# Which loads a pair of weight buffers is kept for, and one weight unit moved ahead of a block, in a hybrid decoder block on one core

## The chip, the cores and the metric

The kernel runs on one core of one Trainium2 chip. The metric is the device time of one execution in microseconds. The time before is the median of three runs, 1735.49 us (1733.80 to 1738.36).

## The reference, cut to what matters

One decoder layer on 256 tokens of width 2048, in fp32: a SwiGLU feed-forward, a mixer, and a second SwiGLU feed-forward, each on a normalised input and added to the residual, and a last norm. The change lies in the two feed-forwards, whose three weights have a hidden width of 5632.

```python
def swiglu_ffn(x, w_gate, w_up, w_down):
    return (jax.nn.silu(x @ w_gate) * (x @ w_up)) @ w_down

x = x + 0.5 * swiglu_ffn(rms_norm(x, ffn1_norm), ffn1_w_gate, ffn1_w_up, ffn1_w_down)
z = rms_norm(x, mix_norm) @ w_in
...  # convolutions, a linear recurrence, gates: y
x = x + y @ w_out
x = x + 0.5 * swiglu_ffn(rms_norm(x, ffn2_norm), ffn2_w_gate, ffn2_w_up, ffn2_w_down)
return rms_norm(x, final_norm)
```

## The kernel before

Every product of activations and weights is made in three passes of TensorE (PE): an fp32 operand is split into a high part (`hi`, a cast by ScalarE, ACT) and a low part (`lo`, the difference to the high part, by VectorE, DVE), and hi·hi, lo·hi and hi·lo are added up. Activations stand still in the array, weights stream through it. A **unit** of weights is 512 rows by 512 columns, 1 MB, in a tile of 128 x 4 x 512. It is loaded by SyncE's queue (SP) into a `raw` buffer, cast in two halves of 128x1024 by ACT, subtracted as 128x2048 by DVE, and then gives 24 matmuls of 128x512: 16 with the high part, 8 with the low one.

There are two ways to use weights. A **plain unit** (`unit`, then `multiply`) is used as just told. A **block** (`seven`) takes two by two units and needs seven products for them where eight are usual; each is made of one sum or difference of weights (by DVE, in place in the raw buffer) and one of activations. Its products come in the order p0, p4, p5, p6, p2, p3, p1, and its four sums lie in the PSUM banks `a`, `c`, `e` and `d`. The weights are w11, w12, w21, w22. p0 uses w11 itself; then DVE writes w12 - w11 into w11's buffer for p4, then w22 less that for p5, and w22 - w12 into w12's buffer for p6. Rows outside the two by two are added by `usual` steps (`x01`, `x00`), which use the units `b2`, `a2` and so on.

A feed-forward runs its hidden width in five double columns, s = 0 to 4, after a first single column. For each s come a gate block and an up block (tiles `g` and `u` with the number of s), and for s = 0, 2 and 4 a **down stage** (tile `d`), which brings the hidden units that are ready back to the width of 2048. In the first down stage these are three, 0, 1 and 2: `others` is [0] and (m, n) is (1, 2). In the two later ones there are four each. A down stage covers output columns 1 and 2 with a block over (m, n) and columns 0 and 3 with plain units, written (column, unit) here. In the first stage their order is (0,0), (0,2), (3,0), (0,1), the block, (3,2), (3,1).

Raw buffers come from two pools. `raws` has three and serves everything; `more` (tag `kept`) has two, is there while a feed-forward runs, and holds w11 and w12 of the blocks. The rule for plain units is the one the diff touches:

```python
        if kept is None and extra and not turn_of["hold"]:
            turn_of["raw"] += 1
            kept = turn_of["raw"] % 5 > 2
```

`unit` passes `kept=None`, so that in down stages two plain units of every five go to the `kept` pair. A load waits until its buffer is free, and SP issues its loads in order. The parts `hi` and `lo` have three pairs of buffers in a feed-forward.

`seven` has an argument `whole`. If it is true, p0's bank `a` is copied by ACT into bank `d`, where the last product goes on adding; if not, ACT copies it into a kept tile `s1`, and DVE adds it at the end. The up block of s = 0 has it false.

The order of the instructions on each engine is set by a scheduler when the kernel is built, so the order in the code is not always that of an engine. All engine operations are recorded at one line, L43, the loads at L168 (`load`) and the transposes at L436. Groups are told apart by tiles: `ps_d_a<-lo_d_p,hs` is a matmul of a down block into bank a, with the low part of the weights of a product p and a sum `hs` of activations; `hi_d` and `lo_d` without a letter behind are plain units.

Of the kernel before, what the change touches and what calls it, by code (L numbers as in the profile page):

```python
# [49 lines left out]
def hybrid_block(ctx: ExitStack, tc: tile.TileContext, a: dict, out: bass.AP):  # L50
# [16 lines left out]
    def pump(budget):  # L67

        owed[0] = min(owed[0], 0.0) + budget
        while pending and owed[0] > 0:  # L70
            cost, fn = pending.popleft()
            fn()
            owed[0] -= cost
# [9 lines left out]
    def bank(name):  # L83
        return psum.tile([P, 512], F32, tag="ps", name=name)

    def f32(ap):
        return ap.bitcast(F32)
# [66 lines left out]


    extra = []
    turn_of = {"raw": 0, "split": 0, "hold": False}

    def load(src, name, pieces=((0, UK),), loaded=None, kept=False):
        if kept is None and extra and not turn_of["hold"]:  # L160
            turn_of["raw"] += 1
            kept = turn_of["raw"] % 5 > 2
        if kept:
            raw = extra[1].tile([P, UK, CW], F32, tag="kept", name=f"raw_{name}", bufs=2)
        else:
            raw = raws.tile([P, UK, CW], F32, tag="raw", name=f"raw_{name}")
        for i, e in pieces:
            nc.sync.dma_start(raw[:, i:e, :], src[i * P : e * P].rearrange("(j p) c -> p j c", p=P))  # L168
            if loaded:
                loaded(i)  # L170
        return raw

    def parts_of(raw, name, pieces=((0, 2), (2, UK)), split=None):
        pool, bufs = splits, 2
        if extra:
            turn_of["split"] += 1
            if turn_of["split"] % 3 == 0:
                pool, bufs = extra[0], 1
        hi = pool.tile([P, UK, CW], F32R, tag="hi", name=f"hi_{name}", bufs=bufs)
        lo = pool.tile([P, UK, CW], F32R, tag="lo", name=f"lo_{name}", bufs=bufs)  # L180
        for i, e in pieces:
            if split:
                split(i)
            act.copy(hi[:, i:e, :], raw[:, i:e, :])
            if split:
                dve.tensor_tensor(lo[:, i:e, :], raw[:, i:e, :], f32(hi[:, i:e, :]), op=ALU.subtract)
        if not split:
            dve.tensor_tensor(lo, raw, f32(hi), op=ALU.subtract)
        return [(hi[:, j, :], lo[:, j, :]) for j in range(UK)]

    def unit(src, name):
        return parts_of(load(src, name, kept=None), name)

    def stationary(tile, t):

        return [(tile[:, j, t * P : (t + 1) * P], tile[:, j, S + t * P : S + (t + 1) * P]) for j in range(UK)]
# [148 lines left out]
    def quad(tile):  # L345
        return tile.rearrange("p (j c) -> p j c", j=UK)
# [65 lines left out]
    def ffn(tag, norm, after, opening=False):  # L412
        with (
# [1 line left out]
            tc.tile_pool(name=f"more{tag}", bufs=1, side="right") as mp,  # L415
        ):
            extra.extend((fp, mp))
            turn_of["hold"] = True
            wg, wu, wd = (a[f"ffn{tag}_w_{s}"][0] for s in ("gate", "up", "down"))

            def keep(name, dt=F32):
# [46 lines left out]
            def on_the_way():  # L468
                return [*tiles, *(entry[0] for entry in moving)]
# [3 lines left out]
            units, vs, sf, ready = [], {}, {}, []  # L473
# [196 lines left out]

            (begin if opening else begin_after)()
            xs = list(enumerate(units))[2:]
            turn_of["hold"] = False

            def down(last):
                us = sorted(set(hidden) | {tile[0] for tile in on_the_way()})
                others, (m, n) = us[:-2], us[-2:]
                end = last and tag == 2

                def update(c, t, *parts):  # L680
                    xr = xres[:, t, c * CW : (c + 1) * CW]
                    for p in parts:
                        dve.scalar_tensor_tensor(xr, p, 0.5, xr, op0=ALU.mult, op1=ALU.add)
                    if last:
                        after(c, t)

                side = {c: [bank(f"ps_d{tag}_{m}_{c}_{t}") for t in range(NT)] for c in (0, 3)}

                def add_units(c, units):
                    blks = [  # L690
                        (u, unit(wd[u * UK * P : (u + 1) * UK * P, c * CW : (c + 1) * CW], f"d{tag}_{m}_{c}_{u}"))
                        for u in units
                    ]
                    assert not {tile[0] for tile in on_the_way()} & set(units)
                    groups = [[0], [1]] if end and units == [n, m] else [[0, 1]]
                    for ts in groups:
                        for u, blk in blks:
                            multiply(
                                [(side[c][t], stationary(hidden[u], t), u == us[0], u == m) for t in ts], blk
                            )  # L700
                            pump(1.5 / len(groups))
                    if units[-1] == m and not (end and c == 0):
                        Engine.pinned = end
                        for t in range(NT):
                            update(c, t, side[c][t])

                sh, got, rest = {}, {}, []

                def block_sums():
                    return seven_of(  # L710
                        sh, hidden[m], hidden[n],
                        {(t, i): turned[u, t] for t in range(NT) for i, u in ((0, m), (1, n))},
                        quad(keep(f"hspare{tag}_{m}")),
                        [[quad(keep(f"hs{tag}_{m}_{i}_{z}", F32R)) for z in range(2)] for i in range(4)],
                    )

                def add(t, b, ps, tiles):
                    got[t, b] = [ps] + tiles
                    if (0, b) in got and (1, b) in got:
                        for i in range(NT):  # L720
                            update(2 - b, i, *got[i, b])

                for c, u in [(0, u) for u in others + [n]] + [(3, u) for u in others]:
                    add_units(c, [u])
                    if not on_the_way() and not rest:
                        rest.append(block_sums())
                add_units(0, [m])

                def within(i):
                    if i == 0:  # L730
                        rest.pop()()
                    elif i == 1 and end:
                        for t in range(NT):
                            update(0, t, side[0][t])

                if tag == 1 and m == 5:
                    prepare()
                seven(
                    wd, (m, n), (2 * CW, CW), sh, [(u, hidden[u]) for u in others], f"d{tag}_{m}", keep, add,
                    within,  # L740
                )
                for units in [[n, m]] if end else [[n], [m]]:
                    add_units(3, units)
                hidden.clear()
                turned.clear()

            for s in range(5):
                cs = (CW + 2 * s * CW, 2 * CW + 2 * s * CW)
                sg = {}

                def total(ps, tiles):
                    for p in tiles[1:]:
                        dve.tensor_tensor(tiles[0], tiles[0], p, op=ALU.add)
                    if not tiles:
                        return ps
                    dve.tensor_tensor(tiles[0], ps, tiles[0], op=ALU.add)
                    return tiles[0]

                def gate(t, n, ps, tiles):
                    g = total(ps, tiles)  # L760
                    sg[t, n] = tiles[0] if tiles else keep(f"z{tag}_{s}")
                    act.activation(sg[t, n], g, AF.Silu)

                def up(t, n, ps, tiles):
                    dve.tensor_tensor(sg[t, n], total(ps, tiles), sg[t, n], op=ALU.mult)
                    turn_hidden(1 + 2 * s + n, t, sg[t, n], s % 2 == 0)

                def meanwhile(i):
                    if s == 0 and not opening and i != 1:
                        (sums, lambda: normalise(3))[i // 2]()  # L770

                seven(wg, (0, 1), cs, sf, xs, f"g{tag}_{s}", keep, gate, meanwhile, ready.pop() if ready else None,
                      s > 0 and (tag, s) != (1, 3))
                seven(wu, (0, 1), cs, sf, xs, f"u{tag}_{s}", keep, up, whole=s > 0)
                if s % 2 == 0:
                    down(s == 4)
            extra.clear()
# [45 lines left out]
    with tc.tile_pool(name="mixer", bufs=1) as mp, tc.tile_pool(name="mixw", bufs=2) as mw:  # L823
# [197 lines left out]
        for c in range(NC_D):  # L1021
            cs = slice(c * CW, (c + 1) * CW)
# [96 lines left out]
```

## Time and profile before

| | before |
|---|---|
| median of 3 runs | 1735.49 us (1733.80 to 1738.36) |
| the profiled execution | 1735.05 us |
| its span, mean granted clock of PE | 1733.1 us, 0.998 |
| PE, PE's weight loads | 99%, 82% of the span |
| DVE, ACT | 85%, 66% |
| moved by DMA | 354.75 MB, mean 205 GB/s |

The span is the time from the first to the last instruction of the profiled execution; the execution is longer by what lies around it. Shares are busy time over the span. A line of the timeline has its start, its length, the engine, the line of the code, the operation, the tile written and those read, the shape, how many instructions were joined (x), and in brackets how long the engine had been idle before and on whom it waited. In SP's lines the length is the time from the issue to the landing of the joined loads.

### The profile page before, as it was taken

The numbers are of one execution on the slowest core, as the hardware profiler recorded it, in microseconds if no ns is written. First come the engines' busy times: TensorE is split into PE (matmuls) and PEld (weight loads), VectorE is DVE, ScalarE is ACT, GpSimd is POOL, SyncE is SP. The second block draws the span as 40 slices with busy tenths as digits, with TensorE's granted clock in tenths as the row PEclk, the third lists the DMA queues.
The fourth block names the chain that finished last, engine by engine and source line by source line (L and its number), as shares of the span: only waits on it lengthen the run. The fifth ranks groups of instructions, "written<-read, shape, count | busy, mean of one in ns | idle before, by whom it ended". The sixth has DMA issues, their size and how long they took to land. (4 is left out here: it accounts for less than half of the span.)

```text
span 1733.1 us, 20143 instructions
## 1 busy us (share of the span) xinstructions
PE 1708.6 (99%) x7859; PEld 1417.9 (82%) x7859; DVE 1472.5 (85%) x1212; ACT 1136.4 (66%) x1433; POOL 6.9 (0%) x32
## 2 busy tenths in 40 slices
PE   8999999999999999999999999999999999999998
PEld 6888788888888888888888888787787887888886
DVE  7997998979799878687986668989799878889786
ACT  6867567775568676575655556686567665567764
POOL 1000000000000000000000000000000000000000
PEclk9999999999999999999999999999999999999999
DMA  8666557585567684556556664684577657576853
GB/s 297 203 217 185 202 199 217 197 266 194 186 211 232 212 249 152 191 170 194 179 187 207 226 200 134 214 264 164 179 233 227 203 187 243 194 213 200 242 202 114
DMA packets 220383, 354.75 MB, mean 205 GB/s; under 512 B 52100, under 2 KB 54528, under 8 KB 220160
## 3 DMA queue, kind: packets, MB, share of 16 engines
q1 hardware_dynamic: 219824, 352.36, 62.8%
q8 instruction: 61, 1.00, 0.2%
q10 hardware_dynamic: 144, 1.05, 0.1%
q14 instruction: 34, 0.28, 0.0%
q0 software_dynamic: 320, 0.07, 0.0%
HBM read 339.82 MB, written 2.10 MB: 197 GB/s over the span
## 5 line engine op out<-in xcount | busy, mean ns | idle before, releaser
L43 DVE TENSOR_TENSOR lo_u_p<-raw_u,hi_u_p 128x2048 fp32r<-128x2048 f32 x70 | 159.3, 2287 | 20.5 <-ACT hi_u_p L43 20.1
L43 ACT CAST hi_u_p<-raw_u 128x1024 fp32r<-128x1024 f32 x140 | 141.8, 1047 | 53.3 <-DVE raw_u L43 16.8
L43 DVE TENSOR_TENSOR lo_g_p<-raw_g,hi_g_p 128x2048 fp32r<-128x2048 f32 x66 | 150.1, 2286 | 25.0 <-ACT hi_g_p L43 24.9
L43 ACT CAST hi_g_p<-raw_g 128x1024 fp32r<-128x1024 f32 x132 | 132.7, 1047 | 54.6 <-DVE raw_g L43 28.6
L43 PE MATMUL ps_d<-hi_d,h 128*128 128x512 f32 x704 | 167.4, 389 | 0.0
L43 PEld LDWEIGHTS ps_d<-hi_d,h 128*128 128x128 f32 x704 | 132.0, 188 | 27.7 <-DVE h L43 0.3
L43 PE MATMUL ps_in<-xT_nm,hi_in 128*128 128x512 f32 x640 | 153.8, 391 | 0.0
L43 ACT CAST hi_d_p<-raw_d 128x1024 fp32r<-128x1024 f32 x84 | 85.4, 1047 | 77.6 <-DVE raw_d L43 34.2
L43 PEld LDWEIGHTS ps_in<-xT_nm,hi_in 128*128 128x128 f32 x640 | 117.3, 188 | 22.9 <-ACT tha L43 0.4
L43 DVE TENSOR_TENSOR lo_d<-raw_d,hi_d 128x2048 fp32r<-128x2048 f32 x44 | 100.4, 2289 | 32.7 <-ACT hi_d L43 32.6
L43 ACT CAST hi_in<-raw_in 128x1024 fp32r<-128x1024 f32 x80 | 80.0, 1045 | 66.3 <-PE ps_in L43 45.9
L43 DVE TENSOR_TENSOR lo_in<-raw_in,hi_in 128x2048 fp32r<-128x2048 f32 x40 | 91.4, 2287 | 35.3 <-ACT hi_in L43 32.9
L43 ACT CAST hi_u_x<-raw_u 128x1024 fp32r<-128x1024 f32 x80 | 80.9, 1046 | 46.5 <-PE ps_u_c L43 23.2
L43 DVE TENSOR_TENSOR lo_d_p<-raw_d,hi_d_p 128x2048 fp32r<-128x2048 f32 x42 | 95.9, 2287 | 15.3 <-ACT hi_d_p L43 15.3
L43 DVE TENSOR_TENSOR raw_u<-raw_u,raw_u 128x2048 f32<-128x2048 f32 x40 | 91.6, 2290 | 13.5 <-DMA raw_u<-in_ffn_w_up_dram 12.9
L43 ACT CAST hi_d<-raw_d 128x1024 fp32r<-128x1024 f32 x88 | 88.5, 1045 | 22.3 <-PE ps_d_d L43 9.8
L43 ACT CAST hi_g_x<-raw_g 128x1024 fp32r<-128x1024 f32 x80 | 81.1, 1046 | 31.7 <-PE ps_g_c L43 11.5
L43 DVE TENSOR_TENSOR lo_g_x<-raw_g,hi_g_x 128x2048 fp32r<-128x2048 f32 x40 | 91.4, 2286 | 2.4 <-ACT hi_g_x L43 2.1
L43 DVE TENSOR_TENSOR lo_u_x<-raw_u,hi_u_x 128x2048 fp32r<-128x2048 f32 x40 | 91.5, 2287 | 2.2 <-ACT hi_u_x L43 2.1
L43 DVE TENSOR_TENSOR raw_g<-raw_g,raw_g 128x2048 f32<-128x2048 f32 x37 | 84.5, 2287 | 7.6 <-DMA raw_g<-in_ffn_w_gate_dram 7.3
L43 PE MATMUL ps_d<-lo_d,h 128*128 128x512 f32 x352 | 87.3, 389 | 0.0
L43 PEld LDWEIGHTS ps_in<-xT_nm,lo_in 128*128 128x128 f32 x640 | 82.2, 191 | 3.2
(395 smaller groups left out, 3650.4 us busy)
## 6 DMA issues: line engine op xcount, KB each, us to landing
raw_d<-in_ffn_w_down_dram SPq DMA_DIRECT2D x88, 1024.0 KB, 5.4
raw_u<-in_ffn_w_up_dram SPq DMA_DIRECT2D x87, 1024.0 KB, 5.3
raw_g<-in_ffn_w_gate_dram SPq DMA_DIRECT2D x86, 1024.0 KB, 5.4
raw_in<-in_w_in_dram SPq DMA_DIRECT2D x40, 1024.0 KB, 5.1
raw_o<-in_w_out_dram SPq DMA_DIRECT2D x16, 1024.0 KB, 5.1
xres<-in_x_dram SPq DMA_DIRECT2D x4, 512.0 KB, 7.6
raw_u<-in_ffn_w_up_dram SPq DMA_DIRECT2D x2, 512.0 KB, 9.4
raw_g_first<-in_ffn_w_gate_dram SPq DMA_DIRECT2D x1, 1024.0 KB, 12.1
```

Source lines behind the costliest of these rows:

```text
L43: ins = getattr(self.engine, name)(*args, **kwargs)
```

## The change

Three things change. The rule above goes: plain units always take one of the three buffers of `raws`, and the `kept` pair holds w11 and w12 of blocks alone. In a down stage with one other unit, which is the first one of each feed-forward, the unit (3, n) stands ahead of the block in the place of behind it. And the up block of s = 0 takes the default `whole=True`, the copy into bank `d`. Line numbers after the first hunk move by three or four: loads are at L165 and transposes at L432.

```diff
@@ -154,12 +154,9 @@
     extra = []
-    turn_of = {"raw": 0, "split": 0, "hold": False}
+    turn_of = {"split": 0}
 
     def load(src, name, pieces=((0, UK),), loaded=None, kept=False):
-        if kept is None and extra and not turn_of["hold"]:
-            turn_of["raw"] += 1
-            kept = turn_of["raw"] % 5 > 2
         if kept:
...
     def unit(src, name):
-        return parts_of(load(src, name, kept=None), name)
+        return parts_of(load(src, name), name)
...
-            turn_of["hold"] = True
...
-            turn_of["hold"] = False
...
-                for c, u in [(0, u) for u in others + [n]] + [(3, u) for u in others]:
+                ahead = [n] if len(others) == 1 else []
+                for c, u in [(0, u) for u in others + [n]] + [(3, u) for u in others + ahead]:
                     add_units(c, [u])
...
-                for units in [[n, m]] if end else [[n], [m]]:
+                for units in [[n, m]] if end else [[u] for u in (n, m) if u not in ahead]:
                     add_units(3, units)
...
-                seven(wu, (0, 1), cs, sf, xs, f"u{tag}_{s}", keep, up, whole=s > 0)
+                seven(wu, (0, 1), cs, sf, xs, f"u{tag}_{s}", keep, up)
```

On PE, before, in the first feed-forward's first down stage from the unit (3,0) to the block's p0 (`ps_d1_1_3_0` is the bank of column 3 for the first half of the tokens, `hi_d1_1_3_0` the high part of unit 0 of column 3; the last number only numbers the tiles):

```order
L43 MATMUL ps_d1_1_3_0_1145<-hi_d1_1_3_0_1226,h1_0_708 128x512 x8
L43 MATMUL ps_d1_1_3_1_1146<-hi_d1_1_3_0_1226,h1_0_708 128x512 x8
L43 MATMUL ps_d1_1_3_0_1145<-lo_d1_1_3_0_1227,h1_0_708 128x512 x4
L43 MATMUL ps_d1_1_3_1_1146<-lo_d1_1_3_0_1227,h1_0_708 128x512 x4
L43 MATMUL ps_d1_1_0_0_1143<-hi_d1_1_0_1_1273,h1_1_1216 128x512 x8
L43 MATMUL ps_d1_1_0_1_1144<-hi_d1_1_0_1_1273,h1_1_1216 128x512 x8
L43 MATMUL ps_d1_1_0_0_1143<-lo_d1_1_0_1_1274,h1_1_1216 128x512 x4
L43 MATMUL ps_d1_1_0_1_1144<-lo_d1_1_0_1_1274,h1_1_1216 128x512 x4
L43 MATMUL ps_d1_1_a_1304<-hi_d1_1_p0_1320,h1_1_1216 128x512 x8
```

And after, from the end of the unit (3,0) on:

```order
L43 MATMUL ps_d1_1_3_1_1144<-lo_d1_1_3_0_1225,h1_0_708 128x512 x4
L43 MATMUL ps_d1_1_3_0_1143<-hi_d1_1_3_2_1271,h1_2_1114 128x512 x8
L43 MATMUL ps_d1_1_3_1_1144<-hi_d1_1_3_2_1271,h1_2_1114 128x512 x8
L43 MATMUL ps_d1_1_3_0_1143<-lo_d1_1_3_2_1272,h1_2_1114 128x512 x4
L43 MATMUL ps_d1_1_3_1_1144<-lo_d1_1_3_2_1272,h1_2_1114 128x512 x4
L43 MATMUL ps_d1_1_0_0_1141<-hi_d1_1_0_1_1302,h1_1_1214 128x512 x8
L43 MATMUL ps_d1_1_0_1_1142<-hi_d1_1_0_1_1302,h1_1_1214 128x512 x8
L43 MATMUL ps_d1_1_0_0_1141<-lo_d1_1_0_1_1303,h1_1_1214 128x512 x4
L43 MATMUL ps_d1_1_0_1_1142<-lo_d1_1_0_1_1303,h1_1_1214 128x512 x4
L43 MATMUL ps_d1_1_a_1333<-hi_d1_1_p0_1349,h1_1_1214 128x512 x8
```

The 24 matmuls of (3,2) now stand between (3,0) and (0,1); behind the block only (3,1) is left.

On SP, before, the loads of the second feed-forward's down stage of s = 2 (`raw_d2_5_0_3` is the plain unit (0,3), `raw_d2_5_50` and `raw_d2_5_51` are the block's w11 and w12, `raw_d2_5_31` its b2, `raw_d2_5_61` its w22):

```order
L168 DMA raw_d2_5_0_6_10593<-in_ffn2_w_down_dram 128x4x512
L436 DMA_TRANSPOSE u2_g2_2_10048<-plane2_10490 128x8x128
L168 DMA raw_d2_5_3_3_10640<-in_ffn2_w_down_dram 128x4x512
L168 DMA raw_d2_5_0_5_10702<-in_ffn2_w_down_dram 128x4x512
L436 DMA_TRANSPOSE z2_2_10207<-plane2_10551 128x8x128
L436 DMA_TRANSPOSE z2_2_10226<-plane2_10590 128x8x128
L168 DMA raw_d2_5_31_10743<-in_ffn2_w_down_dram 128x4x512
L168 DMA raw_d2_5_61_10745<-in_ffn2_w_down_dram 128x4x512
L168 DMA raw_d2_5_41_10747<-in_ffn2_w_down_dram 128x4x512
L168 DMA raw_d2_5_50_10739<-in_ffn2_w_down_dram 128x4x512
L168 DMA raw_d2_5_51_10741<-in_ffn2_w_down_dram 128x4x512
```

And after, the start of the same stage:

```order
L165 DMA raw_d2_5_50_10735<-in_ffn2_w_down_dram 128x4x512
L165 DMA raw_u2_2_30_10242<-in_ffn2_w_up_dram 128x4x512
L165 DMA raw_d2_5_0_3_10512<-in_ffn2_w_down_dram 128x4x512
L165 DMA raw_d2_5_51_10737<-in_ffn2_w_down_dram 128x4x512
L432 DMA_TRANSPOSE u3_g2_2_10100<-plane2_10431 128x8x128
L165 DMA raw_d2_5_0_4_10550<-in_ffn2_w_down_dram 128x4x512
L432 DMA_TRANSPOSE u2_g2_2_10044<-plane2_10486 128x8x128
```

The block's two first weights were the last of these to be issued and are now the first, ahead of and next to the stage's first plain unit.

## The prediction

> **What bounds the kernel now.** I read the page first, for the engine that has no room, then the waits of TensorE's weight loads, then busy time and clock by stretches of 50 us, and last the timeline where those two show a loss.
>
> ```profile
> PE 1708.6 (99%) x7859; PEld 1417.9 (82%) x7859; DVE 1472.5 (85%) x1212; ACT 1136.4 (66%) x1433; POOL 6.9 (0%) x32
> core 0: 1733.1 us, clock 0.998
> ```
>
> TensorE (PE) is busy 99% of the span, so only time in which PE stands still or runs slowly can be won. The span is 1733.1 us and the execution took 1735.05, so 1.95 us lie around it; I carry the sum in the execution's own time, which is 0.44 us below the median of 1735.49. The pace of PE is read from two starts:
>
> ```profile
> 151.01 3.79 PE L43 MATMUL ps_d<-hi_d,h 128*128 128x512 f32 x16
> 154.64 1.98 PE L43 MATMUL ps_d<-lo_d,h 128*128 128x512 f32 x8
> ```
>
> Sixteen matmuls take 154.64 - 151.01 = 3.63 us, 0.227 each. A plain unit has 16 + 8 of them, 5.44 us. The list of the waits (total us, count, mean us) names who keeps PE waiting there:
>
> ```profile
> PEld ps_d_a L43 <- DVE lo_d_p L43: 3.8, 2, 1.9
> PEld ps_d_c L43 <- ACT s_d L43: 3.1, 2, 2.2
> ```
>
> These are four waits only, all in down stages. The windows (busy time and count of PE, PEld, DVE, ACT, POOL, then the granted clock) show where they lie:
>
> ```profile
> 150.00:200.00 50.00, 47.95 (x201) 38.25 (x200) 46.46 (x34) 31.14 (x36) 0.00 (x0) 0.97 0.55 183
> 178.80:182.20 3.40, 3.40 (x10) 2.62 (x9) 3.40 (x3) 1.60 (x3) 0.00 (x0) 0.50 0.31 96
> 1150.00:1200.00 50.00, 48.40 (x212) 39.22 (x211) 43.72 (x34) 37.59 (x45) 0.00 (x0) 1.00 0.63 189
> 1192.00:1196.00 4.00, 2.40 (x11) 1.50 (x10) 4.00 (x4) 2.76 (x4) 0.00 (x0) 1.00 0.69 247
> ```
>
> 150 to 200 holds the first feed-forward's first down stage, 1150 to 1200 the second one's. At full pace 50 us hold 220 matmuls; there are 201 and 212, so 50 - 201 x 0.227 = 4.4 us and 50 - 212 x 0.227 = 1.9 us are lost. The timeline shows how the 4.4 come about:
>
> ```profile
> 173.37 2.12 PE L43 MATMUL ps_d_a<-hi_d_p,hs 128*128 128x512 f32 x8
> 175.56 2.29 DVE L43 TENSOR_TENSOR lo_d_p<-raw_d,hi_d_p 128x2048 fp32r<-128x2048 f32 x1
> 175.78 0.50 PE L43 MATMUL ps_d_c<-hi_d_p,hs 128*128 128x512 f32 x1 [0.29 <-ACT hi_d_p L43]
> 177.90 1.34 PE L43 MATMUL ps_d_a<-lo_d_p,hs 128*128 128x512 f32 x4 [1.61 <-DVE lo_d_p L43]
> 179.03 3.19 PE L43 MATMUL ps_d_c<-hi_d_p,hs 128*128 128x512 f32 x7
> ```
>
> Product p5's high part ends at about 173.37 + 8 x 0.227 = 175.2. Its low part is made by VectorE (DVE) from 175.56 to 177.85, and PE goes on at 177.90. Right after that the clock falls to 0.50 for 3.40 us, and seven matmuls take 3.19 us where 7 x 0.227 = 1.6 would do: 1.6 us of the 4.4 are clock, the rest waiting. DVE is busy 46.46 of these 50 us, so it is DVE that is late, not a load.
>
> [...] The clock of 0.50 follows waits of at most 1.61 us, and at 1192 to 1196, where PE is busy only 2.40 of 4.00 us, it stays at 1.00. [...]
>
> **The change part by part.**
>
> *The unit ahead of the block.* No work is added: 24 matmuls, two casts and one subtraction move from behind the first down stage's block to ahead of it. PE gets 5.44 us of work before the block, while DVE, which has the block's low parts in its queue, gets 2.29. So DVE gains 5.44 - 2.29 = 3.1 us of lead at p5, against a lateness of 177.90 - 175.2 less the one matmul of 0.227 put in between (at 175.78), 2.5 us. The stall at p5 goes with some 0.6 us to spare, and with it what I take to be the reason for the fall of the clock. I take the full 4.4 us of this stage and the 1.9 us of the second feed-forward's.
>
> What is late next: PE reaches the following gate block 4.4 us earlier, and DVE must follow.
>
> ```profile
> 207.41 2.28 DVE L43 TENSOR_TENSOR lo_g_p<-raw_g,hi_g_p 128x2048 fp32r<-128x2048 f32 x1
> 212.04 1.07 PE L43 MATMUL ps_g_c<-lo_g_p,xs 128*128 128x512 f32 x4
> 216.81 2.29 DVE L43 TENSOR_TENSOR lo_g_p<-raw_g,hi_g_p 128x2048 fp32r<-128x2048 f32 x1 [2.12 <-ACT hi_g_p L43]
> 220.20 1.07 PE L43 MATMUL ps_g_a<-lo_g_p,xs 128*128 128x512 f32 x4
> ```
>
> p4's low part is ready at 209.69 now and used at 212.04: 2.35 us of margin. p5's is ready at 219.10 and used at 220.20: 1.10. After the change they are wanted at 207.6 and 215.8. If DVE recovers nothing of its idle time it is late by 2.1 and 3.3 us; if it recovers all of its 50 - 46.46 = 3.5 us and the 2.12 us at 216.81, by nothing. Followed by hand in DVE's new order it recovers nearly all of the first, but not all of the second, since that cast waits for a subtraction on DVE itself: p4 comes out even and p5 0.4 to 0.9 late. I take 1.0 us given back, with 0 and 3.3 as ends. In the second feed-forward PE comes only 1.9 us earlier and DVE has 50 - 43.72 = 6.3 us idle: 0.3 given back, ends 0 and 1.9.
>
> *Two buffers for blocks alone.* A block's first two weights, w11 and w12, now find their buffers free as soon as the block before has let go of them, since no plain unit of a down stage sits there. Where before they did not:
>
> ```profile
> 1214.88 12.13 SPq L168 DMA_DIRECT2D raw_g<-in_ffn_w_gate_dram  x2
> 1220.92 2.29 DVE L43 TENSOR_TENSOR raw_g<-raw_g,raw_g 128x2048 f32<-128x2048 f32 x1 [3.87 <-DMA raw_g<-in_ffn_w_gate_dram]
> 1235.14 2.15 PE L43 MATMUL ps_g_a<-hi_g_p,xs 128*128 128x512 f32 x8 [1.21 <-ACT hi_g_p L43]
> 1405.96 5.37 SPq L168 DMA_DIRECT2D raw_d<-in_ffn_w_down_dram  x3
> 1413.74 2.00 ACT L43 CAST hi_d_p<-raw_d 128x1024 fp32r<-128x1024 f32 x2 [6.89 <-DMA raw_d<-in_ffn_w_down_dram]
> 1415.78 2.29 DVE L43 TENSOR_TENSOR lo_d_p<-raw_d,hi_d_p 128x2048 fp32r<-128x2048 f32 x1 [4.84 <-ACT hi_d_p L43]
> 1431.34 1.89 PE L43 MATMUL ps_d_c<-hi_d_x,h 128*128 128x512 f32 x7 [1.74 <-ACT s_d L43]
> 661.27 0.96 PE L43 MATMUL ps_d_c<-hi_d_x,h 128*128 128x512 f32 x3 [0.47 <-ACT s_d L43]
> ```
>
> DVE idles 3.87 us for w12 of the second feed-forward's g_1 block, and PE pays 1.21 us fourteen microseconds on. At 1413 ScalarE (ACT) waits 6.89 us for w11 and DVE 4.84 behind it, and PE pays 1.74 when the copy s_d comes late. The stall of 0.47 at 661 has the same shape in the first feed-forward's last down stage. With w11 and w12 loaded a stage earlier all three go: 1.21 + 1.74 + 0.47 = 3.4 us. Their end on the other side is 0, if another operand of the same product is as late.
>
> *Three buffers for the plain units.* They had five in rotation, now three. The rows are the two groups of a unit's splitting, the median landing of a down load, and one small addition, in this order from the groups, the DMA issues and the timeline:
>
> ```profile
> L43 DVE TENSOR_TENSOR lo_d<-raw_d,hi_d 128x2048 fp32r<-128x2048 f32 x44 | 100.4, 2289 | 32.7 <-ACT hi_d L43 32.6
> L43 ACT CAST hi_d<-raw_d 128x1024 fp32r<-128x1024 f32 x88 | 88.5, 1045 | 22.3 <-PE ps_d_d L43 9.8
> raw_d<-in_ffn_w_down_dram SPq DMA_DIRECT2D x88, 1024.0 KB, 5.4
> 152.87 0.69 DVE L43 TENSOR_TENSOR hs<-hspare,hs 128x512 fp32r<-128x512 f32 x1
> ```
>
> One turn of a buffer costs 5.4 + 2 x 1.05 + 2.29 = 9.8 us, and with three of them PE uses it up in 3 x 5.44 = 16.3 us, so 6.5 us are to spare. The tightest load is the block's w22: it is issued when the unit two ahead of the block has been split, and DVE needs it after one more such split, one addition of 0.69, p0's split and a subtraction, 3 x 2.29 + 0.69 = 7.6 us later. The landing of 5.4 leaves 2.2. I cost it at 0; SP's queue is in order, and nothing in it stands behind a load that waits longer than before.
>
> *The first up block.* It now carries product p0 into bank d by a copy on ACT, in place of a copy into a kept tile, and DVE's addition of that tile goes: 0.69 us of DVE twice, in a stretch where PE does not wait for it. Ends -1.4 and 0; I take 0.
>
> **The sum.** 4.4 - 1.0 + 1.9 - 0.3 + 3.4 = 8.4 us less. 1735.05 - 8.4 = 1726.7 in the execution's own time, and 1727.1 against the median. Less than 0.3%, 5.2 us, can hardly be told from no change: faster is below 1730.3, slower above 1740.7.
>
> **The rivals.**
>
> *The stall only moves.* DVE's work between the down stage's start and the gate block is the same before and after, and DVE is nearly full there. If it recovers none of its idle time, the gate block pays up to 3.3 us in the first feed-forward and the 1.9 in the second, and if the three late loads turn out to be held by DVE too, only 4.4 + 1.9 - 3.3 - 1.9 = 1.1 us are left: 1734.4. With the loads' 3.4 it is 1731.0. For it speaks that 46.46 of 50 us; against it the 3.5 us of idle time, which sits between casts and subtractions of the very block that now gets its lead. Chance 0.17, no measurable change.
>
> *Three buffers are too few (slower).* Two loads issued together took 12.13 us until the second had landed (the row at 1214.88). If w22 goes out together with the load ahead of it, it lands 12.1 - 7.6 = 4.5 us late, and DVE, being in order, holds p4's low part behind the subtraction that waits for it. In the two first down stages DVE has no slack and PE pays 4.5 each time. In the other four PE has some cover: half of DVE's 4.84 us of idle at 1415.78, 2.4, leaves 2.1 each. 2 x 4.5 + 4 x 2.1 = 17.4 us: 1744.5. It decides from a landing of 7.6 us on; to end above the time before, 8.4 us have to be lost. For it speaks that row; against it that the load ahead of w22 gets its buffer one split (2.29 us) earlier, and that the DMA share in the window's row of 150 to 200 is 0.55. [...] Chance 0.09.
>
> *The slow clock comes and goes.* If the runs behind the median did not have the stretch at 0.50, or if it comes after another short wait, 1.6 us less is won: 1728.7. This lies within the forecast's side.
>
> *The change doesn't do what it says.* If the move ahead is swallowed because PE then waits for the moved unit's own split, PE loses at (3,2) what it wins at p5. Only the loads' 3.4 us are left then: 1732.1. It is counted with the first rival.
>
> **How the numbers follow.** The forecast, with or without the clock, has 0.74, the stall that moves 0.17, too few buffers 0.09. Faster takes 0.73 (the forecast less its upper edge), the same 0.18, slower 0.09. The likeliest time is 1727.1. Below it the ends are nothing given back (-1.3), DVE's two additions (-1.4), and the spread of the three runs of before, 1733.8 to 1738.36, about half of which moves a median: 1722.5. Above it the range takes in the first rival whole and a little noise: 1736.0, which leaves out the slow rival.
>
> **What would show it right or wrong.** Right: no wait for lo_d_p above 0.5 us in the first down stages, a clock of 1.00 in the window after them, windows of 150 to 200 and 1150 to 1200 with 215 or more matmuls; waits of PE for lo_g_p of up to 0.9 in the first g_1 block; no wait of ACT or DVE for a load of w11 or w12. Wrong: waits of PE for lo_g_p or hi_g_p above 2 us just after the down stage (the stall moved), or DVE subtractions that wait several us for a load of raw_d in every down stage (too few buffers).

## The result, and the profile after

| | before | after |
|---|---|---|
| median in the comparison | 1734.64 us (4 runs, 1733.58 to 1738.36) | 1723.53 us (4 runs, 1723.29 to 1723.74) |
| ratio, 95% interval | | 0.9932 [0.9915, 0.9949] |
| the profiled execution, its span | 1735.05, 1733.1 us | 1723.6, 1721.7 us |

The kernel became 11.1 us faster by the medians; 8.4 were forecast, and 1723.53 lies in the range of 1722.5 to 1736.0, near its lower end. The windows of the kernel after (columns as in the prediction) show where PE now stands:

```profile
150.00:200.00 50.00, 50.00 (x222) 41.24 (x221) 49.44 (x35) 29.34 (x35) 0.00 (x0) 1.00 0.61 211
178.80:182.20 3.40, 3.40 (x17) 2.65 (x16) 3.40 (x4) 2.29 (x4) 0.00 (x0) 1.00 0.86 297
200.00:250.00 50.00, 50.00 (x222) 41.24 (x221) 46.31 (x25) 31.84 (x38) 0.00 (x0) 1.00 0.50 172
640.00:690.00 50.00, 50.00 (x222) 41.40 (x221) 43.84 (x29) 31.24 (x41) 0.00 (x0) 1.00 0.46 162
1100.00:1150.00 50.00, 48.61 (x213) 39.36 (x212) 44.39 (x26) 34.06 (x39) 0.00 (x0) 1.00 0.70 230
1150.00:1200.00 50.00, 50.00 (x222) 41.25 (x221) 44.68 (x34) 35.59 (x43) 0.00 (x0) 1.00 0.59 192
1200.00:1250.00 50.00, 50.00 (x222) 41.27 (x221) 46.07 (x29) 30.18 (x34) 0.00 (x0) 1.00 0.64 217
1400.00:1450.00 50.00, 50.00 (x223) 41.39 (x221) 44.00 (x27) 28.20 (x32) 0.00 (x0) 1.00 0.62 212
```

Before, those of them that the prediction did not show were:

```profile
200.00:250.00 50.00, 50.00 (x222) 41.41 (x221) 44.79 (x24) 29.12 (x34) 0.00 (x0) 1.00 0.59 201
640.00:690.00 50.00, 49.53 (x219) 40.68 (x218) 42.61 (x27) 29.97 (x39) 0.00 (x0) 1.00 0.46 160
1100.00:1150.00 50.00, 49.34 (x216) 39.80 (x215) 44.91 (x26) 33.62 (x39) 0.00 (x0) 1.00 0.68 226
1200.00:1250.00 50.00, 48.79 (x214) 39.41 (x213) 43.17 (x28) 24.50 (x27) 0.00 (x0) 1.00 0.56 193
1400.00:1450.00 50.00, 48.26 (x213) 39.64 (x212) 42.23 (x30) 28.17 (x34) 0.00 (x0) 1.00 0.51 179
```

A window in which PE waits for nothing holds 222 matmuls. The counts give the account, at 0.227 us each: the first down stages 201 to 222 and 212 to 222, 4.8 and 2.3 us; the second feed-forward's gate block g_1 214 to 222, 1.8 us; its down stage of s = 2 213 to 223, 2.3 us; the stage at 660 219 to 222, 0.7 us; and on the other side the second feed-forward's first up block, 216 to 213, 0.7 us lost. That is 49 matmuls, 11.1 us; the two profiled executions lie 11.45 us apart.

The product p5 of the first down stage, where PE had waited 1.61 us and the clock had then fallen to 0.50, reads after:

```profile
175.39 2.28 DVE L43 TENSOR_TENSOR lo_d_p<-raw_d,hi_d_p 128x2048 fp32r<-128x2048 f32 x1
178.20 1.98 PE L43 MATMUL ps_d_a<-hi_d_p,hs 128*128 128x512 f32 x8
179.40 2.28 DVE L43 TENSOR_TENSOR lo_d_p<-raw_d,hi_d_p 128x2048 fp32r<-128x2048 f32 x1
180.01 1.07 PE L43 MATMUL ps_d_a<-lo_d_p,hs 128*128 128x512 f32 x4
```

DVE finishes p5's low part at 177.67 and PE uses it at 180.01: 2.3 us of lead where it had been late. In the gate block that follows, DVE's lead over PE is down to a trace:

```profile
204.49 2.28 DVE L43 TENSOR_TENSOR lo_g_p<-raw_g,hi_g_p 128x2048 fp32r<-128x2048 f32 x1
207.32 1.07 PE L43 MATMUL ps_g_c<-lo_g_p,xs 128*128 128x512 f32 x4
213.29 2.29 DVE L43 TENSOR_TENSOR lo_g_p<-raw_g,hi_g_p 128x2048 fp32r<-128x2048 f32 x1 [2.12 <-ACT hi_g_p L43]
215.71 1.12 PE L43 MATMUL ps_g_a<-lo_g_p,xs 128*128 128x512 f32 x4
```

p4's low part has 207.32 - 206.77 = 0.55 us to spare, p5's 215.71 - 215.58 = 0.13.

### The profile page after: what moved, and what is told of

It reads as the page before. It is cut to its first block, busy times and chain, and to the rows that moved or that the text cites. A ratio compares the mean times of both kernels' runs of the same rounds, so it can differ in the third digit from the quotient of the medians.

```text
span 1721.7 us, 20143 instructions
## 1 busy us (share of the span) xinstructions
PE 1703.6 (99%) x7859; PEld 1417.2 (82%) x7859; DVE 1473.1 (86%) x1210; ACT 1135.7 (66%) x1433; POOL 6.9 (0%) x32
## 4 chain that ended last, share of the span: by engine, by line
PE 90%; DVE 4%; ACT 1%; issue 0%; DMA 0%; DVEq 0%; ACTq 0%
PE ps_d L43 14%; PE ps_in L43 13%; PE ps_u_a L43 8%; PE ps_g_a L43 8%; PE ps_u_c L43 6%; PE ps_g_c L43 6%; PE ps_d_a L43 5%; PE ps_o L43 5%; PE ps_g_d L43 4%; PE ps_u_d L43 3%; PE ps_d_c L43 3%; PE ps_u_e L43 3%; PE ps_g_e L43 3%; PE ps_d_d L43 3%; PE ps_d_e L43 2%; DVE lo_g_p L43 1%
```

## The experiments

**The three parts, each alone.** First the moved unit alone.

```diff
+                ahead = [n] if len(others) == 1 else []
-                for c, u in [(0, u) for u in others + [n]] + [(3, u) for u in others]:
+                for c, u in [(0, u) for u in others + [n]] + [(3, u) for u in others + ahead]:
```

> The kernel before with the unit (3, n) ahead of the block alone; the rule for plain units and the up block's tile stay as before. Theory (VectorE is late in the first down blocks, the moved unit gives it time): PE full from 150 to 200 and from 1150 to 1200 (222 matmuls each, from 201 and 212), clock 1.00; that is 4.7 + 2.3 us less, about 1728. The losses near 660, 1233 and 1429 stay (0.6, 1.4, 1.9 us). Rival (the loads of w11 and w12 that come early are what freed the first down blocks): 150 to 200 still loses 3 us or more, and the time is 1732 or above.

It took 1729.11 us (5 runs), ratio 0.9969 [0.9956, 0.9982]: 4.9 us less than the 1733.99 of its comparison, where the theory had 7.0. The windows of this run:

```profile
150.00:200.00 50.00, 49.39 (x218) 40.42 (x217) 47.84 (x34) 30.66 (x36) 0.00 (x0) 1.00 0.60 202
1150.00:1200.00 50.00, 50.00 (x222) 41.24 (x221) 43.65 (x34) 34.71 (x43) 0.00 (x0) 1.00 0.64 194
1200.00:1250.00 50.00, 48.22 (x210) 38.43 (x209) 42.60 (x28) 27.86 (x33) 0.00 (x0) 1.00 0.58 202
1400.00:1450.00 50.00, 48.23 (x213) 39.60 (x212) 41.96 (x27) 26.68 (x31) 0.00 (x0) 1.00 0.51 176
```

Both first down stages are nearly full (218 and 222) with no change to the loads, so the rival that early loads had freed them falls. The late loads keep their price (213 from 1400 to 1450), and in the second g_1 block it grows from 8 missing matmuls to 12: there the stall moved, much as the first rival of the prediction had it. The likely cause is w12: DVE's subtraction that waits for it starts at 1216.84, 4.1 us earlier than before (1220.92), while PE came some 6 us earlier (17 and 10 matmuls more in the two first down stages).

Then the buffers alone.

```diff
     def unit(src, name):
-        return parts_of(load(src, name, kept=None), name)
+        return parts_of(load(src, name, kept=False), name)
```

> The kernel before without the rule for plain units alone: they take the three buffers, the pair holds w11 and w12 of blocks; the unit (3, n) stays behind the block. Theory: the losses near 660, 1233 and 1429 go (0.4 + 1.9 + 2.1 us by windows of the kernel after), the stalls in the first down stages stay (4.8 and 1.9 us): about 1730.5. Rival (loads freed the first down blocks): these go as well, 1724 to 1726. Second rival (the slow stretch of the clock is chance): the first down stage waits for lo_d_p 2 us as before but the clock stays at 1.00: 1.6 us less than the theory, 1729.

It took 1727.59 us (4 runs), ratio 0.9958 [0.9941, 0.9974]: 6.4 us less than its comparison, where the theory had about 5. Its first down stage and the windows of the two late loads:

```profile
150.00:200.00 50.00, 47.57 (x206) 37.97 (x205) 47.09 (x34) 31.75 (x37) 0.00 (x0) 1.00 0.56 192
178.45 1.21 PE L43 MATMUL ps_d_a<-lo_d_p,hs 128*128 128x512 f32 x4 [1.61 <-DVE lo_d_p L43]
179.50 1.78 PE L43 MATMUL ps_d_c<-hi_d_p,hs 128*128 128x512 f32 x7
1200.00:1250.00 50.00, 50.00 (x222) 41.42 (x221) 46.53 (x30) 29.78 (x34) 0.00 (x0) 1.00 0.61 218
1400.00:1450.00 50.00, 50.00 (x222) 41.42 (x221) 45.51 (x29) 28.41 (x32) 0.00 (x0) 1.00 0.57 195
```

The wait for p5's low part is there to the hundredth, 1.61 us, but the clock stays at 1.00 and the seven matmuls behind it take 1.78 us, not 3.19. So the second rival holds: after a wait of the same length the slow clock comes in one execution and not in another (0.50 before and 1.00 here over the 3.40 us from 178.80). The two late loads are gone, 222 each.

Last the copy into bank d alone.

```diff
-                seven(wu, (0, 1), cs, sf, xs, f"u{tag}_{s}", keep, up, whole=s > 0)
+                seven(wu, (0, 1), cs, sf, xs, f"u{tag}_{s}", keep, up)
```

> The kernel before with the copy into bank d in the up block of s = 0 alone. Theory: no gain; VectorE has 0.69 us less to do twice where PE doesn't wait for it. PE's loss at the second feed-forward's first up block (0.69 + 0.29 us before, 0.97 + 0.75 after) is expected to grow by 0.7 if the copy causes it: 1735 to 1736. Rival: the addition that goes is what gives VectorE its lead into the first down stage: 1733 to 1734, with the stall at 177.9 shorter by 0.7 us.

It took 1737.44 us (10 runs), ratio 1.0014 [1.0004, 1.0024]: a little slower, against both. Its trace:

```profile
1217.43 2.00 ACT L43 CAST hi_g_p<-raw_g 128x1024 fp32r<-128x1024 f32 x2 [5.07 <-DMA raw_g<-in_ffn_w_gate_dram]
1200.00:1250.00 50.00, 46.18 (x201) 36.67 (x200) 41.54 (x25) 23.79 (x26) 0.00 (x0) 1.00 0.54 187
1428.00:1438.00 10.00, 7.99 (x29) 6.10 (x28) 9.79 (x9) 8.32 (x11) 0.00 (x0) 0.83 0.37 113
```

With one addition less the scheduler placed the load of the second g_1's w11 two loads later in SP's queue; it landed after ACT had waited 5.07 us, and the g_1 window lost 13 matmuls more than before. That it would have come in time had the pair not been shared with plain units is argued, not shown. At 1428 to 1438 a stall that before has at full clock met the slow one (0.83 over 10 us, 1.00 before). In the first down stage the wait at p5 is gone, but PE waits 2.10 us at p4 in its place (at 168.86), and 150 to 200 holds 204 matmuls, 201 before.

**What the copy is worth beside the other two.** The kernel after without it:

```diff
-                seven(wu, (0, 1), cs, sf, xs, f"u{tag}_{s}", keep, up)
+                seven(wu, (0, 1), cs, sf, xs, f"u{tag}_{s}", keep, up, whole=s > 0)
```

> The kernel after with the up block of s = 0 as before (kept tile and addition, no copy into bank d). Theory: the lead of the moved unit doesn't hang on it: within 1 us of 1723.5; if the copy causes the 0.7 us more at the second feed-forward's first up block, 1722.8. Rival (VectorE is so full from 150 to 200, 49.4 of 50 us, that 0.69 more shows): PE waits 0.5 us or more again in the first down or gate block: 1724.5 to 1725.

It took 1725.64 us (4 runs, 1725.05 to 1726.10), ratio 0.9947 [0.9932, 0.9962]. Here the rival is right, with a time a little above its own. To see whether it is DVE's 0.69 us or something else in the copy, that work alone was put back into the kernel after:

```diff
                 def up(t, n, ps, tiles):
+                    if s == 0 and (t, n) == (0, 0):
+                        idle = keep(f"idle{tag}")
+                        dve.tensor_tensor(idle, ps, sg[t, n], op=ALU.add)
```

> The kernel after with one more addition of 128x512 on VectorE (0.69 us, into a tile that nobody reads) in the up block of s = 0 of each feed-forward, where the addition of the kept tile stood before. The copy into bank d stays. Theory (the copy into bank d helps because it takes 0.69 us from VectorE while that engine is the limit): the losses of the run without the copy come back, 0.8 us each from 200 to 250 and from 1200 to 1250 and 0.6 at 1187: 1725 to 1726. Rival (it helps through ScalarE's order or the tiles that come free): no change, 1723.5.

It took 1725.60 us (4 runs, 1723.91 to 1725.79), ratio 0.9940 [0.9920, 0.9961]. The gate block of the first feed-forward in this run, and two windows of the second one:

```profile
205.46 2.28 DVE L43 TENSOR_TENSOR lo_g_p<-raw_g,hi_g_p 128x2048 fp32r<-128x2048 f32 x1
207.79 0.77 PEld L43 LDWEIGHTS ps_g_c<-lo_g_p,xs 128*128 128x128 f32 x4 [0.48 <-DVE lo_g_p L43]
216.60 0.53 PEld L43 LDWEIGHTS ps_g_a<-lo_g_p,xs 128*128 128x128 f32 x3 [0.51 <-DVE lo_g_p L43]
1150.00:1200.00 50.00, 49.45 (x218) 40.47 (x217) 43.18 (x34) 34.59 (x43) 0.00 (x0) 1.00 0.64 202
1200.00:1250.00 50.00, 49.83 (x219) 40.60 (x218) 46.82 (x30) 30.75 (x35) 0.00 (x0) 1.00 0.62 217
```

And without the copy, the same windows:

```profile
1150.00:1200.00 50.00, 49.58 (x218) 40.58 (x217) 43.50 (x33) 34.17 (x41) 0.00 (x0) 1.00 0.62 198
1200.00:1250.00 50.00, 49.81 (x219) 40.60 (x218) 46.86 (x30) 30.50 (x36) 0.00 (x0) 1.00 0.63 217
```

218 and 219 in both: an addition of 0.69 us that nobody reads does what the missing copy does. In the gate blocks the weight loads wait for p4's and p5's low parts, the two places that the prediction named for the time given back: DVE starts p4's low part at 205.20 without the copy and at 205.46 with the addition put back, at 204.49 in the kernel after. From 1150 to 1200 the loss stands elsewhere, at a matmul that waits 0.42 and 0.55 us for ACT's copy s_d. In both runs the scheduler also changed the order of ACT and SP (the transpose of `s_g` is issued at 147.95 and 148.21, at 144.17 in the kernel after), so DVE's 0.69 us and the order that comes with them are not told apart.

The copy in the first feed-forward alone:

```diff
+                seven(wu, (0, 1), cs, sf, xs, f"u{tag}_{s}", keep, up, whole=s > 0 or tag == 1)
```

> The kernel after with the copy into bank d in the first feed-forward's up block of s = 0 alone; the second one has its kept tile and addition as before. Theory: the second first up block loses 0.5 us less (1.55 from 1100 to 1150, not 2.11), and its first down stage and gate block lose 1.4 more (0.83 and 0.79 us from 1150 and 1200 on, as in the run without the copy): 1724.4. Rival (the copy is worth nothing in the second feed-forward): 1723.0.

It took 1724.64 us (4 runs, 1723.48 to 1726.31), ratio 0.9938 [0.9917, 0.9958], near the theory's 1724.4 but too spread to hold it against 1723.0. Its second feed-forward does what the theory says: 216, 217 and 219 matmuls from 1100, 1150 and 1200 on, where the kernel after has 213, 222 and 222. Its profiled execution was the slowest, and its first feed-forward shows why the spread: up to 1115 us its instructions are those of the kernel after, and yet the first down stage and g_1 lost some matmuls. ACT's first copy of turned hidden units in the kernel after:

```profile
132.25 1.34 ACT L43 COPY plane<-u_g 128x1024 uint16<-128x1024 uint16 x1
```

And in this run, with what follows:

```profile
133.90 1.35 ACT L43 COPY plane<-u_g 128x1024 uint16<-128x1024 uint16 x1 [1.42 <-DMA u_g<-plane]
136.19 2.29 DVE L43 TENSOR_TENSOR lo_d<-raw_d,hi_d 128x2048 fp32r<-128x2048 f32 x1 [4.06 <-ACT hi_d L43]
200.00:250.00 50.00, 49.81 (x219) 40.61 (x218) 46.32 (x26) 30.47 (x36) 0.00 (x0) 1.00 0.52 182
```

The transpose that this copy reads landed 6.0 us after its issue in place of 4.5; ACT waited for it with its next cast behind, and DVE's chain ran 1.6 us later from there. The 2.21 and 1.24 us of the next expectation are the lengths of SP's lines for the transpose after it. They are not times to landing, though the part on the profile before reads SP's lines so: a line's length runs from the start of its first issuing instruction to the end of its last one, and that transpose landed 7.7 us after its issue here and 6.3 in the kernel after. The kernel after was therefore run once more, to see how often that happens.

> The kernel after, unchanged, beside the other runs of its family. In the run with the copy in the first feed-forward alone, the same instructions up to that point ran VectorE 1.6 us later, since one transpose before the first down stage took 2.21 us and not 1.24; the median is asked for over more executions. Theory (the copy into bank d is worth 1 to 2 us because VectorE has 0.69 us less to do): 1723.3 to 1724.0 again, below 1725.6 and 1725.6 of the runs that take it away or put its work back. Rival (the 2 us between them are this transpose, late in some executions): 1724.5 to 1725.7, with single executions from 1723.3 to 1725.8.

It took 1723.23 us (5 runs: 1723.04, 1723.15, 1723.23, 1723.67, 1724.47), ratio 0.9938 [0.9925, 0.9951]. The theory holds for the median, the rival for one execution: the one of 1724.47 was profiled, with a transpose that landed 7.4 us after its issue (6.3 in the first trace) and 218 matmuls from 200 to 250. So the copy is worth some 2 us (1723.23 and 1723.53 with it, 1725.64 and 1725.60 without it or with its work put back). These medians stand in different comparisons, and the intervals of their ratios overlap, so the counts carry the argument. In the second feed-forward they agree: 222 from 1150 and 222 from 1200 on in both profiled executions of the kernel after, 217 or 218 and 219 in the three runs where the copy is missing there or its work is put back. In the first, g_1 lost three matmuls in the two where the copy is missing or undone, though their transposes landed no later (6.0 us after the issue, 6.3 in the kernel after), and with the copy in the two executions with a late transpose.

**How far three buffers are from too few.** Two in place of three, in the whole program:

```diff
-    raws = ctx.enter_context(tc.tile_pool(name="raws", bufs=3, side="right"))
+    raws = ctx.enter_context(tc.tile_pool(name="raws", bufs=2, side="right"))
```

> The kernel after with two buffers in the pool that plain units and the other block loads share, in place of three, in the whole program. It asks how far three are from too few. A buffer's turn of 9.8 us against 2 x 5.44 = 10.9 us of PE for plain units leaves 1.1 us there; in a block w22 and w21 are held while other units must pass through the other buffer. Theory (three leave 2 us or more at the tightest load): with two every block is late, PE loses some us in each of the 26 blocks: 1780 or above, waits for loads of raw_d, raw_g and raw_u of several us on VectorE. Rival (loads have far more room than 2 us): under 1735.

It took 1874.42 us (4 runs), ratio 1.0806 [1.0778, 1.0834]. The list of waits (total, count, longest), first of ACT for loads, then of PE's weight loads for ACT:

```profile
ACT hi_g_x L43 <- DMA raw_g<-in_ffn_w_gate_dram: 57.4, 19, 5.9
ACT hi_u_x L43 <- DMA raw_u<-in_ffn_w_up_dram: 52.0, 25, 4.3
ACT hi_d L43 <- DMA raw_d<-in_ffn_w_down_dram: 48.6, 24, 7.6
PEld ps_u_d L43 <- ACT hi_u_x L43: 28.2, 18, 4.0
PEld ps_u_a L43 <- ACT hi_u_p L43: 22.6, 39, 2.6
PEld ps_d L43 <- ACT hi_d L43: 8.1, 9, 2.0
```

With three, ACT's wait for the loads of plain down units is 3.5 us over four waits:

```profile
ACT hi_d L43 <- DMA raw_d<-in_ffn_w_down_dram: 3.5, 4, 1.2
```

One buffer fewer costs 150 us. It is mostly ACT that waits for loads, those of plain units and of the steps outside the two by two, and not, as expected, DVE; PE pays at the products of the blocks and at those steps, and little at plain units (8.1 us). Three are enough; the slower rival of the prediction was about a real edge, one buffer away.

**The unit ahead of the block in other stages too.**

```diff
-                ahead = [n] if len(others) == 1 else []
+                ahead = [] if end else [n]
```

> The kernel after with the unit (3, n) ahead of the block also in the down stages of s = 2 and, in the first feed-forward, of s = 4. Theory (the moved unit helps only where VectorE is late in the block): nothing is late there after the change (0.01 to 0.36 us lost from 650 to 700 and 1400 to 1450), so nothing is won: within 1 us of 1723.5. Rival (a unit ahead gives lead wherever it stands, also for the gate block that follows): 1 us less or more for each stage moved, 1721 or below. Other side: the gate block after it gets its first casts later, up to 0.8 us lost in each: 1725.

It took 1735.62 us (10 runs), ratio 1.0004 [0.9990, 1.0018]: all of the gain is gone, and not at a gate block. The down stages are full; the loss stands where the first feed-forward ends and the mixer begins:

```profile
700.00:750.00 50.00, 43.25 (x227) 36.77 (x226) 28.68 (x50) 24.52 (x43) 0.45 (x10) 0.90 0.38 124
711.25 5.53 PE L43 MATMUL ps_in<-xT_nm,hi_in 128*128 128x512 f32 x16 [2.02 <-DVE xT_nm L43]
721.59 0.79 PE L43 MATMUL ps_in<-xT_nm,hi_in 128*128 128x512 f32 x2 [2.02 <-DVE xT_nm L43]
```

The kernel after has 293 matmuls in the same window. The mixer's input is turned (`xT_nm`) in pieces that `pump` takes up after each plain unit; with one unit fewer behind the block some of them seem to be left over. PE waits 6.8 us in four waits, and with the three of 2.02 us the clock falls for a while (0.83 over each of the stretches of 10 us from 710, 720 and 730 on, 1.00 from 700 to 710 with the wait of 0.70 us): sixteen matmuls take 5.53 us behind the wait at 711.25, and 3.93 behind that of 0.70. Waits and clock together are some 11.5 of the 12 us. That the units behind the block are this cover was then tried by leaving the last stages alone:

```diff
-                ahead = [n] if len(others) == 1 else []
+                ahead = [] if last else [n]
```

> The kernel after with the unit (3, n) ahead of the block in the down stages of s = 0 and s = 2, but not in the last one of either feed-forward. Theory (the 12 us lost by having it ahead everywhere lie in the first feed-forward's last stage alone, where the unit behind the block is what PE does while the mixer's input is turned; at s = 2 the move is worth nothing): 1723.0 to 1724.5, 293 matmuls from 700 to 750 as after, not 227. Rival (moving it at s = 2 costs as well): 1726 or above.

It took 1723.86 us (5 runs), ratio 0.9931 [0.9917, 0.9944], with 290 matmuls from 700 to 750. So at s = 2 the move is worth nothing in the median, and the 12 us lie in the last stage alone. The profiled execution did pay at the gate block behind the moved stage (PE waits 1.40 us at 539.93, 213 matmuls from 500 to 550, 218 in the kernel after); the run with the unit ahead everywhere did not (0.36 us, 218).

**What is left at p4.** In the kernel after DVE makes w22 - w12 (for p6) ahead of p4's low part, and PE loses about 1 us at the start of the gate blocks of s = 2 and 4 (218 matmuls from 250 to 300). The subtraction was pinned behind that low part, in all blocks and then in these four:

```diff
         product_of(4, w11, c, True)
+        tc.keep_in_program_order(nc.vector.tensor_tensor(w12, w22, w12, op=ALU.subtract))
...
-        dve.tensor_tensor(w12, w22, w12, op=ALU.subtract)
```

> The kernel after, with the subtraction w22 - w12 (for p6) pinned behind p4's low part on VectorE in every block. In the kernel after it stands ahead of that low part, 2.29 us, where PE waits for p4's low part 0.5 to 1.0 us at the start of the gate blocks of s = 2 and s = 4. Theory (VectorE's order at p4 is what is left to win): these four waits go, 0.97 + 0.98 + 0.99 + 0.99 us: about 1719.6. Rival (the low part waits for its cast, not for the subtraction): 1723.5. Other side: pinning moves p6's cast back and PE waits there, 0.5 us in some of the 26 blocks: 1728 or above.

> The same pinning in the four gate blocks of s = 2 and s = 4 alone. Theory: the same four waits go and nothing else moves: about 1719.6. Rival (the low part waits for its cast): 1723.5.

They took 1745.07 us (ratio 1.0063 [1.0048, 1.0079]) and 1725.75 us (0.9953 [0.9936, 0.9970]): both theories fall, and of the first expectation the other side is right (1728 or above). In the second, in the first feed-forward, the window of the gate block gains two matmuls (220 from 218) and that of the up block behind it loses five (217 from 222):

```profile
250.00:300.00 50.00, 49.95 (x220) 40.77 (x219) 43.52 (x27) 37.79 (x42) 0.00 (x0) 1.00 0.74 210
300.00:350.00 50.00, 49.45 (x217) 40.25 (x216) 45.01 (x25) 32.91 (x39) 0.00 (x0) 1.00 0.62 211
```

The wait moved on to the up block's own p4 (PE waits 0.41 us for its low part at 331.14). In the second feed-forward the gate blocks gain nothing (217 from 218) and the up blocks lose two. In the run with all blocks pinned, the scheduler reordered PE and ACT as well, and what of its 22 us comes from which block was not followed up. No kernel of these beats the one after.

## Why the prediction was right, and where it was not

*The moved unit* was right in mechanism and nearly in size: 4.4 and 1.9 us were forecast for the two first down stages, 4.8 and 2.3 came, and the run with the move alone, with 3.9 and 2.3, shows that it is the move; the rest of the first stage's came with the other parts. p5 has 2.3 us of lead where the working gave 0.6; with the move alone it has 1.28 (ready at 179.53, used at 180.81), part of which is a wait of PE of 0.61 us for ACT's copy s_d.

*The time given back* (1.3 us) did not come in the kernel after, but its place and its size were nearly right for a kernel without the copy: there g_1 loses three matmuls (0.7 us) in each feed-forward, 1.4 in all, at p4 and p5 as worked out, and so it does with DVE's work put back. That the kernel after does not pay comes from the next term, which failed.

*The first up block* was costed at nothing, "in a stretch where PE does not wait for it". DVE is nearly full from there to the gate block (49.44 of 50 us from 150 to 200 after), so 0.69 us saved ahead of it arrives at p4 and p5, where the margins are 0.55 and 0.13 us. It is worth some 2 us here, net of 0.7 us that the second feed-forward's first up block lost (216 to 213); alone it is worth less than nothing. Without it the kernel takes 1725.64, 8.35 us below the 1733.99 of its comparison. That this is the forecast's 8.4 to the tenth is luck: the interval of the ratio goes from 6.6 to 11.8 us, and the late loads below were sized 1.4 us too small.

*The late loads* were put at 1.21 + 1.74 + 0.47 = 3.4 us, from the idle time that stands in brackets. They were worth 1.8 + 2.3 + 0.7 = 4.8 by the count of matmuls. The bracket is all the idle time that PE shows (50 - 48.79 = 1.21 us from 1200 to 1250, 50 - 48.26 = 1.74 from 1400 to 1450); the rest of the missing matmuls stands as longer ones (the eight at 1230.88 and the eight at 1235.14 take 2.14 and 2.15 us, where eight take 1.98 at full pace), which the count has and the bracket leaves out.

*Three buffers for the plain units* were costed at nothing, and that held: ACT waits 3.5 us in all for loads of plain down units, and the down stages' windows are full all the same.

*The sum.* Against the 8.4 us the moved unit brought 0.8 more, the late loads 1.4 more, the 1.3 given back were not paid, and 0.7 was lost at the second first up block: 11.2, about the 11.1 measured. The forecast held in direction and range with terms that were too small on the whole. One of its signs did not hold: DVE still waits 2.87 us for w12 of that up block, in its subtraction at 1109.54 (2.59 before, at 1114.14).

*The rivals.* The stall that only moves was seen once, where w12 stays late. Too few buffers did not happen, and the row that spoke for it was misread: the 12.13 us at 1214.88 join two loads that were not issued together. The first landed after 6.0 us, where DVE's wait ends at 1220.92, and the second was issued only at 1226.64. Likewise the third number in the prediction's list of waits is the longest wait, not the mean. The slow clock that comes and goes is shown: a wait of 1.61 us was followed by it before (0.50 from 178.80 to 182.20) and not with the buffers alone (1.00), so that such a wait can bring the slow clock and need not.

## What to carry to other kernels

Where one engine feeds another with no slack, work is not free because nobody waits for it at that place: follow it to the next place where the margin is small, and price it there. Moving work ahead of a hard stretch takes cover from what stands behind it; moved in the two stages that lacked it, it won 5 us, moved in the last stage too it cost 12. And a buffer pool shared between the first operands of a block and filler work can make the time of those operands hang on a small shift of the schedule: one addition less made the kernel slower by a ratio of 1.0014 while the pair was shared, and won some 2 us beside the other two changes. And a wait should be counted by the work that is missing in a window, not only by the idle time in brackets.

## What the hardware showed beside that

Behind waits of PE of nearly the same length the granted clock fell in some places and not in others. Of five waits of 1.60 to 1.85 us in these runs it fell behind one (1.61 at 177.90 before) and stayed at 1.00 behind four (1.60 at 1194.49 and 1.74 at 1431.34 before, 1.61 at 178.45 with the buffers alone, 1.85 at 1226.28 with the copy alone). With five others, of 2.01 to 2.10 us, it fell: 2.10 at 168.86 and 2.01 at 1431.86 with the copy alone, and the three of 2.02 with the unit ahead everywhere, each with a clock of 0.83 over 10 us. Ten waits are too few for a rule. Where it fell, seven matmuls took 3.19 us, 1.6 more than 7 x 0.227, and sixteen took 5.53, 1.6 more than the 3.93 at a clock of 1.00: such a stall cost some 1.6 us beyond its own length.

The four runs of before spread over 4.8 us (1733.58 to 1738.36), the nine of the kernel after, whose large stalls are gone, over 1.4 (1723.04 to 1724.47); that the clock makes the difference was not measured.

In three executions of the same instructions the two transposes that SP issues among 1 MB loads ahead of the first down stage landed at different times after their issue: 4.5 and 6.3 us in the first trace of the kernel after, 6.0 and 7.7 with the copy in the first feed-forward alone, and the second of them after 7.4 in the second trace of the kernel after. With the kernel's leanest margin of 0.13 us the later ones cost 0.7 to 0.9 us at g_1 (219 and 218 matmuls from 200 to 250, 222 in the first trace).
